# A transformer trunk's convolution inputs moved into Strassen quads, with weight sums made by adding loads

## The chip, the cores and the metric

The kernel runs on one core of one Trainium2 chip. The metric is the time of one execution on the device in microseconds. Its engines work side by side, each through a queue of its own in the order in which instructions were placed there: TensorE (PE; PEld is its weight load), VectorE (DVE), ScalarE (ACT), GpSimd (POOL), and SyncE (SP), which here only issues loads and stores.

## The reference

Two layers over 512 tokens of width 1024. Each has two half-step feed-forward blocks, a mixer between them, and a gated input embedding. The mixer's core:

```python
u = rmsnorm(h, mix_norm[i])
b_g, c_g, v_c, q_c, kv_c, k_r, g_conv, g_mla = jnp.split(u @ w_in[i], split_pts, axis=-1)
y_conv = short_conv_branch(b_g, c_g, v_c, conv_w[i], w_conv_out[i])
y_mla = mla_branch(q_c, kv_c, k_r, q_norm[i], kv_norm[i], w_uq[i], w_ukv[i], w_mla_out[i], cos, sin)
merged = jax.nn.sigmoid(g_conv) * y_conv + jax.nn.sigmoid(g_mla) * y_mla
h = h + merged @ w_o[i]
...
z = c_gate * v                       # short_conv_branch; zp is z with two zero rows ahead
y = conv_w[0] * zp[:, 0:seq]         # plus taps 1 and 2
return (b_gate * y) @ w_conv_out
```

The convolution's inputs B, C and V are 512 columns of `w_in` each; the two gates are 1024 each.

## The kernel before

Activations lie as columns by tokens: `h` is eight tiles of 128 x 512. Everything is computed in float32 through a split: a value is cast to a high part (`wh` for weights, on ScalarE) and the rest is taken on VectorE (`wl`), and a product is made of three matmuls (high times high, high times low, low times high). A block of eight 128 x 128 weight tiles is 128 x 1024, 512 KB. `Stream.raw` loads such a block into a buffer `st` (ten of them) on SP's queue; `Stream.split` makes `wh`, `wl` from it (four of each). A plain projection (`proj`) of 128 output columns uses eight tiles and 24 matmuls of 512 columns.

Some weights are multiplied by Strassen's method in Winograd's form. A quad covers four blocks of 128 output columns; it takes four blocks of weights (`a11`, `a21`, `a22`, `a12`) and makes seven products, numbered 1 to 7, instead of eight. A product is 24 matmuls of 256 columns (half of the tokens). `Quad.part(j)` gives the weights of product j: four of the seven are sums of blocks, made on VectorE (1024 columns each). Products 1, 6, 7 and 4 gather in one PSUM bank `b`, 5 and 3 in `c`, 2 in `a`; after products 1, 5 and 6 ScalarE copies the bank away (`c1`, `c5`, `c6`), after the others VectorE adds bank and copies, and `done` finishes a quarter. Products 5, 7, 6 and 4 need differences of the activations: `Halved.row(j, xs)` makes, for each of four rows, x and y on ScalarE, and t and u (two halves of 256 columns each) and their splits on both engines. Product 5 needs the t of all four rows.

A mixer `m0` or `m1` runs in this order: two projections `kvp`, the rotary key `krp` (its weights need a memset on GpSimd), the sum for its norm (`m0ps`) and from it r (`rms`), three q projections, then four times C, V and B projections with the convolution of that block and one row of `Halved`, then four quads `g0` to `g3` for the gates, with the convolution's output (`conv_out`) between products from the second on, then attention. The Tile framework's scheduler places instructions on each queue from the order of the program and its own estimates; `issue_after(ins)` puts what a block traces on the engine of `ins` behind it. Names such as `wl100` number the splits over the whole program.

## Time and profile before

| | |
|---|---|
| Median of 3 runs | 2277.63 us (2277.48 to 2277.65) |
| The profiled execution | 2277.8 us, span 2275.7 us |
| TensorE's granted clock in it | 0.999 |
| Busy: PE, PEld, DVE, ACT, POOL | 2266.7, 2058.0, 1816.1, 1163.2, 38.1 us |
| DMA | 223.28 MB, mean 98 GB/s |

A row of a timeline gives the start in microseconds, the busy time, engine, line, operation, the tiles written and read, and how often it follows itself; in brackets the idle time ahead of it and who ended it. Engines overlap the end of one instruction with the start of the next, so the distance of two starts is the pace, and the busy time is a little longer.

### The profile page before, as it was taken

How to read it: one execution, taken by the hardware profiler on the slowest of the kernel's cores; microseconds unless marked ns; L12 is line 12 of the kernel's file. 1: busy time of each engine (PE TensorE's matmuls, PEld its weight loads, DVE VectorE, ACT ScalarE, POOL GpSimd, SP SyncE). 2: the span in 40 equal slices, each digit the busy share in tenths (PEclk: the TensorE clock that was granted, in tenths of full speed). 3: DMA queues.
4: the chain of work that ended last, by engine and by line, in shares of the span. 5: the costliest groups of instructions: out<-in, count | busy, mean ns of one | idle time of the engine just before them, and what ended most of it. 6: DMA issues, size and time to landing. Idle time of an engine off the chain costs nothing.

```text
span 2275.7 us, 34817 instructions
## 1 busy us (share of the span) xinstructions
PE 2266.7 (100%) x14206; PEld 2058.0 (90%) x14206; DVE 1816.1 (80%) x2544; ACT 1163.2 (51%) x1751; POOL 38.1 (2%) x42
## 2 busy tenths in 40 slices
PE   9999999999999999999999999999999999999998
PEld 8999988899888999998899999888998889999987
DVE  8877778877877988877798887767878689878766
ACT  7444445456745644444664444454567465444444
POOL 0000000000200000000000000000001000000000
PEclk9999999999999999999999999999999999999999
DMA  5333343134121333333223333422331214333321
GB/s 195 112 112 95 105 130 102 55 113 130 47 66 56 103 112 111 94 120 122 91 80 97 112 93 118 119 87 74 103 121 47 75 38 138 103 103 93 121 93 38
DMA packets 63375, 223.28 MB, mean 98 GB/s; under 512 B 7280, under 2 KB 7280, under 8 KB 63216
## 3 DMA queue, kind: packets, MB, share of 16 engines
q1 hardware_dynamic: 62640, 220.28, 30.7%
q8 instruction: 111, 1.82, 0.3%
q10 hardware_dynamic: 576, 0.79, 0.1%
q14 instruction: 48, 0.39, 0.1%
HBM read 218.94 MB, written 2.10 MB: 97 GB/s over the span
## 4 chain that ended last, share of the span: by engine, by line
PE 98%; DVE 1%; ACT 0%; issue 0%; DVEq 0%; ACTq 0%
PE a0pd L217 2%; PE a1pd L217 2%; PE b0pd L217 2%; PE b1pd L217 2%; PE b1pd L218 2%; PE b0pd L218 2%; PE a1pd L218 2%; PE a0pd L218 2%; PE b0pd L219 2%; PE a1pd L219 2%; PE a0pd L219 2%; PE b1pd L219 2%; PE m0mop L217 1%; PE m1mop L218 1%; PE m0mop L218 1%; PE e0gp L219 1%
## 5 line engine op out<-in xcount | busy, mean ns | idle before, releaser
L70 ACT CAST wh<-st 128x1024 fp32r<-128x1024 f32 (+1 forms) x458 | 476.8, 1044 | 567.2 <-issue 62.7
L71 DVE TENSOR_TENSOR wl<-st,wh 128x1024 fp32r<-128x1024 f32 (+1 forms) x459 | 555.1, 1211 | 155.0 <-ACT wh L70 154.2
L70 ACT CAST wh<-s 128x1024 fp32r<-128x1024 f32 x98 | 103.0, 1051 | 132.6 <-DVE s L151 8.9
L71 DVE TENSOR_TENSOR wl<-s,wh 128x1024 fp32r<-128x1024 f32 x98 | 119.3, 1218 | 13.5 <-ACT wh L70 13.5
L154 DVE TENSOR_TENSOR st<-st,s 128x1024 f32<-128x1024 f32 x49 | 59.9, 1222 | 1.2
L151 DVE TENSOR_TENSOR s<-s,st 128x1024 f32<-128x1024 f32 x49 | 59.7, 1218 | 0.2
L157 DVE TENSOR_TENSOR st<-st,st 128x1024 f32<-128x1024 f32 x49 | 59.6, 1217 | 0.1
L146 DVE TENSOR_TENSOR s<-st,st 128x1024 f32<-128x1024 f32 x49 | 59.6, 1216 | 0.1
L563 DVE SCALAR_TENSOR_TENSOR h<-b1pd,h 128x512 f32<-128x512 f32 x40 | 27.5, 688 | 10.4 <-PE b1pd L219 10.4
L563 DVE SCALAR_TENSOR_TENSOR h<-b0pd,h 128x512 f32<-128x512 f32 x40 | 27.5, 687 | 9.1 <-PE b0pd L219 9.1
L563 DVE SCALAR_TENSOR_TENSOR h<-a1pd,h 128x512 f32<-128x512 f32 x40 | 27.5, 687 | 7.6 <-PE a1pd L219 7.5
L563 DVE SCALAR_TENSOR_TENSOR h<-a0pd,h 128x512 f32<-128x512 f32 x40 | 27.4, 685 | 6.4 <-PE a0pd L219 6.4
L107 POOL MEMSET wh<- 128x256 f32 x4 | 1.1, 312 | 1189.7 <-DVE wl L71 1189.7
L988 ACT ACTIVATE e1g<-e1pg,e1r 128x512 f32<-128x512 f32 (+1 forms) x9 | 5.4, 641 | 11.9 <-PE e1pg L950 11.9
L992 DVE TENSOR_TENSOR e1g<-e1g,e1in 128x512 f32<-128x512 f32 (+1 forms) x9 | 5.7, 628 | 7.3 <-ACT e1g L988 7.3
L117 DVE TENSOR_TENSOR kl<-st,kh 128x512 fp32r<-128x512 f32 x8 | 5.3, 688 | 7.4 <-ACT kh L116 7.4
L882 DVE TENSOR_TENSOR m1g<-m1mop,m1g 128x512 f32<-128x512 f32 x8 | 5.5, 689 | 5.9 <-PE m1mop L219 5.9
L882 DVE TENSOR_TENSOR m0g<-m0mop,m0g 128x512 f32<-128x512 f32 x8 | 5.5, 689 | 5.5 <-PE m0mop L219 5.5
L300 ACT ACT_TABLE_LOAD x7 | 9.0, 1283 | 0.1
L287 DVE TENSOR_TENSOR e1acc<-e1acc,e1sq 128x512 f32<-128x512 f32 x7 | 4.8, 691 | 4.8 <-ACT e1sq L286 4.3
L709 DVE TENSOR_TENSOR m1g<-m1cop,m1g 128x512 f32<-128x512 f32 x8 | 5.5, 687 | 2.0 <-PE m1cop L219 2.0
L709 DVE TENSOR_TENSOR m0g<-m0cop,m0g 128x512 f32<-128x512 f32 x8 | 5.5, 687 | 2.0 <-PE m0cop L219 2.0
(11249 smaller groups left out, 8792.5 us busy)
## 6 DMA issues: line engine op xcount, KB each, us to landing
st<-in_weights SPq DMA_DIRECT2D x406, 512.0 KB, 3.5
h<-in_x SPq DMA_DIRECT2D x8, 256.0 KB, 5.3
st<-in_weights SPq DMA_DIRECT2D x7, 256.0 KB, 5.3
out<-e1d SPq DMA_DIRECT2D x4, 256.0 KB, 2.1
out<-fh SPq DMA_DIRECT2D x3, 256.0 KB, 2.2
e0pi<-in_p SPq DMA_DIRECT2D x2, 256.0 KB, 3.7
e1pi<-in_p SPq DMA_DIRECT2D x2, 256.0 KB, 3.7
fg<-in_final_row SPq DMA_DIRECT2D x2, 256.0 KB, 4.4
```

The lines of the kernel that those rows point to most:

```text
L70: self.nc.scalar.copy(hi[:, w], src[:, w])
L71: last = self.nc.vector.tensor_tensor(lo[:, w], src[:, w], hi[:, w].bitcast(F32), ALU.subtract)
L146: tt(self.s, self.a21, self.a22, ALU.add)
L151: tt(self.s, self.s, self.a11, ALU.subtract)
L154: tt(self.a12, self.a12, self.s, ALU.subtract)
L157: tt(self.a11, self.a11, self.a21, ALU.subtract)
L217: nc.tensor.matmul(ps, wh, vh, start=first, stop=False)
L218: nc.tensor.matmul(ps, wh, vl, start=False, stop=False)
L219: nc.tensor.matmul(ps, wl, vh, start=False, stop=last)
L563: nc.vector.scalar_tensor_tensor(h[m], ps, 0.5, h[m], ALU.mult, ALU.add)
L709: nc.vector.tensor_tensor(gates[m], ps, gates[m], ALU.mult)
L882: nc.vector.tensor_tensor(t, mla_ps[m], t, ALU.mult)
```

## The change

The convolution's C, V and B columns become quads 0, 1 and 2 of the mixer, ahead of the gates (quads 3 to 6), so 12 projections become 21 products. All four rows of `Halved` are made before that, and the q projections stand between the first products. The mixer's quads use a new class: three of their four weight sums are made by loading a block a second time with addition into the buffer that holds another one, on GpSimd's queue. [...] In each later quad product 5 comes ahead of product 1.

```diff
+class Added(Quad):
+    def __init__(self, W, quarters):
...
+        for q in ("a11", "a21", "a22", "a12"):
+            self.at[q] = len(W.halves)
+            setattr(self, q, W.raw(quarters[q]))
+        self.s = self.a21
+        self.add(self.s, "a22")
+
+    def add(self, t, q):
+        self.W.nc.gpsimd.dma_start(out=t, in_=self.W.src[self.at[q]], accum_op=ALU.add)
+
+    def part(self, j):
+        W = self.W
+        if j == 1:
+            res = W.split(self.a11)
+            self.add(self.a11, "a21")
+            return res
+        if j == 5:
+            res = W.split(self.s)
+            self.add(self.s, "a11")
+            return res
+        if j == 3:
+            W.nc.vector.tensor_tensor(self.a12, self.a12, self.s, ALU.add)
+        return W.split({2: self.a12, 3: self.a12, 6: self.s, 7: self.a11, 4: self.a22}[j])
...
-        qt = lat_scale(lat_in(o_q, QL, "q"), "q")
-        kvt = lat_norm(*kvt, "kv")
         krt = rope(krn, cosT, sinT, name + "kr")
-        ys = Halved("mix", l, name)
...
+        ys = Halved("mix", l, name, True)
+        rows = []
+        for k in range(KD // 2):
+            _, last = ys.row(k, xs)
+            rows.append((last, split_to.cast))
         r2 = G(name + "r2")
         nc.vector.tensor_tensor(r2, r, r, ALU.mult)
-        for k in range(CONV // P):
-            ps = proj(W.col("w_in", l, o_c + k * P, D), xs, f"{name}Cp{k}")
...
-            yc.append(split(y, f"{name}yc{k}"))
-            ys.row(k, xs)
-            if k == 1:
-                qt = lat_norm(*qt, "q", SCALE)
...
+        def columns(n):
+            c0 = (o_c, o_v, o_b)[n] if n < N_CONV else o_gc + 4 * (n - N_CONV) * P
+            return [[c0 + (2 * a_ + w) * P for w in range(2)] for a_ in range(2)]
+
+        def conv(n, f, c, src, t):
...
+            if n == 0:
+                nc.vector.tensor_tensor(t, src, r2[:, at].unsqueeze(1).to_broadcast([P, 2, H]), ALU.mult)
+                cs[f, c] = t
+            elif n == 1:
+                for w, k in blocks:
+                    nc.vector.tensor_tensor(zs[k][:, at], src[:, w, :], cs[f, c][:, w, :], ALU.mult)
...
+            else:
+                nc.vector.tensor_tensor(t, src, r[:, at].unsqueeze(1).to_broadcast([P, 2, H]), ALU.mult)
...
-        step = Sevens("w_in", l, name + "g", ys.ys,
-                      lambda n: [[o_gc + (4 * n + 2 * a_ + w) * P for w in range(2)] for a_ in range(2)], gate).step
-        for j in (1, 2, 5, 6, 3):
-            step(0, j)
-        n_last = KD // 2 - 1
+        step = Sevens("w_in", l, name + "g", ys.ys, columns, gate, Added).step
+        step(0, 1)
+        q_block(0)
+        step(0, 2)
+        q_block(1)
+
+        with tc.issue_after(rows[0][0]), tc.issue_after(rows[0][1]):
+            q_block(2)
+        kvt = lat_norm(*kvt, "kv")
+        qt = q_ts, q_sq.parts()
+        with tc.issue_after(rows[1][0]), tc.issue_after(rows[1][1]):
+            step(0, 5)
+        with tc.issue_after(rows[3][0]), tc.issue_after(rows[3][1]):
+            for n, j in ((1, 1), (1, 2), (0, 6), (0, 3)):
+                step(n, j)
+        n_last = N_CONV + KD // 2 - 1
         for n in range(n_last):
...
-            order = [(n + 1, 1), (n, 7), (n + 1, 5), (n, 4)]
-            order += [(n + 1, j) for j in ((6, 2, 7, 3, 4) if n + 1 == n_last else (2, 6, 3))]
+            order = [(n + 1, 5), (n, 7)] + ([(n + 1, 1)] if n else []) + [(n, 4)]
+            order += [(n + 1, j) for j in ((6, 2, 7, 3, 4) if n + 1 == n_last else (2, 6, 3) if n else (6, 3))]
```

How this moves instructions, in layer 0. First VectorE's queue after r. `kvt`, `kvacc` and `kval` are the kv scaling and its sum, `krs` and `krn` the rotary key, `qt` and `qacc` the q scaling and its sum. Before:

```order
L662 TENSOR_TENSOR m0krs_3707<-m0krp_3655,m0krs_3707 64x512
L664 TENSOR_TENSOR m0krn_3706<-m0krs_3707,m0r_3685 64x512 x2
L637 TENSOR_TENSOR m0qt0_3805<-m0qp0_3712,m0r_3685 128x512
L71 TENSOR_TENSOR wl101_3921<-st74_3918,wh101_3920 128x1024
L637 TENSOR_TENSOR m0qt1_3809<-m0qp1_3743,m0r_3685 128x512
L287 TENSOR_TENSOR m0qacc_3807<-m0qacc_3807,m0qsq_3811 128x512
```

Now, from the same rotary key on (`krt` its rotation, t0 and u0 the first row):

```order
L695 TENSOR_TENSOR m0krs_3707<-m0krp_3655,m0krs_3707 64x512
L697 TENSOR_TENSOR m0krn_3706<-m0krs_3707,m0r_3685 64x512 x2
L650 TENSOR_TENSOR m0krt1_3712<-m0krn_3706,cosT_132 128x512
L651 TENSOR_TENSOR m0krt2_3713<-m0krt2_3713,sinT_133 128x512
L429 TENSOR_TENSOR m0t0_3722<-m0x0_3721 128x256
L652 TENSOR_TENSOR m0krt1_3712<-m0krt1_3712,m0krt2_3713 128x512
L445 TENSOR_TENSOR m0t0_3722<-m0y0_3727,m0x0_3721 128x256
L447 SCALAR_TENSOR_TENSOR m0u0_3728<-m0t0_3722,m0x0_3721 128x256
L448 SCALAR_TENSOR_TENSOR m0u0_3728<-m0u0_3728,m0y0_3727 128x256
L241 TENSOR_TENSOR m0t0l_3726<-m0t0_3722,m0t0h_3725 128x512
L241 TENSOR_TENSOR m0u0l_3736<-m0u0_3728,m0u0h_3735 128x512
L71 TENSOR_TENSOR wl100_3950<-st75_3947,wh100_3949 128x1024
```

The split of q block 2's weights (`wl100`) now stands behind the rotation and row 0; rows 1 and 2, the kv norm (`m0kvr`, `m0kvt`) and the split `wl101` of product 5 follow, and then the end of row 3 and what stands ahead of the split `wl102` (quad 1's product 1):

```order
L241 TENSOR_TENSOR m0t3l_3780<-m0t3_3776,m0t3h_3779 128x512
L241 TENSOR_TENSOR m0u3l_3790<-m0u3_3782,m0u3h_3789 128x512
L705 TENSOR_TENSOR m0r2_3793<-m0r_3685 128x512
L711 TENSOR_TENSOR m0qt0_3875<-m0qp0_3844,m0r_3685 128x512
L515 TENSOR_TENSOR m0g0c1_3842<-m0g0a_3879,m0g0c1_3842 128x512
L711 TENSOR_TENSOR m0qt1_3941<-m0qp1_3910,m0r_3685 128x512
L735 TENSOR_TENSOR m0g0c1_3842<-m0g0c1_3842,m0r2_3793 128x512
L711 TENSOR_TENSOR m0qt2_3977<-m0qp2_3946,m0r_3685 128x512
L318 TENSOR_TENSOR m0qacc_3877<-m0qacc_3877,m0qsq_3943 128x512
L71 TENSOR_TENSOR wl102_4042<-st76_4031,wh102_4041 128x1024
```

The q scalings, which stood right behind the rotary key, now stand behind all four rows, and `wl102` behind them. On TensorE's queue, after q block 2, the convolution's first projection followed before:

```order
L219 MATMUL m0qp2_3774<-m0x7h_3582,wl98_3778 128x512
L296 MATMUL m0kvps_3823<-m0kvah_3702,ones_76 128x512
L297 MATMUL m0kvps_3823<-m0kval_3703,ones_76 128x512
L217 MATMUL m0Cp0_3847<-m0x0h_3534,wh99_3850 128x512
L218 MATMUL m0Cp0_3847<-m0x0l_3535,wh99_3850 128x512
```

Now product 5 of quad 0 (bank `m0g0c`) follows, which reads the rows; this is its end and what comes after it:

```order
L491 MATMUL m0g0c_3999<-m0t3l_3780,wh101_4000 128x256
L491 MATMUL m0g0c_3999<-m0t3h_3779,wl101_4001 128x256
L491 MATMUL m0g1b_4040<-m0x0h_3534,wh102_4041 128x256
L491 MATMUL m0g1b_4040<-m0x0l_3535,wh102_4041 128x256
L491 MATMUL m0g1a_4072<-m0x4h_3561,wh103_4073 128x256
L491 MATMUL m0g1a_4072<-m0x4l_3562,wh103_4073 128x256
L491 MATMUL m0g0b_3812<-m0u0h_3735,wh104_4104 128x256
L491 MATMUL m0g0b_3812<-m0u0l_3736,wh104_4104 128x256
L491 MATMUL m0g1b_4040<-m0x0h_3534,wl102_4042 128x256
```

Two matmuls each of three products (quad 1's 1 and 2, quad 0's 6), then the rest of the first, which reads `wl102`. GpSimd's queue held only the memset for the rotary key's weights at this place before:

```order
masks.py:199 ISA
masks.py:199 AFFINE_SELECT ident_80<-ident_80 128x128
L107 MEMSET wh95_3658 128x4x64 x2
L814 TENSOR_SCALAR m0s00e0_5613<-m0s00e0_5613,m0s00sm_5616 128x128
L814 TENSOR_SCALAR m0s00e0_5613<-m0s00e0_5613,m0s00sm_5616 128x384
```

Now adding loads stand around it (`st70` is s of quad 0, `st77` that of quad 1, `st81` that of quad 2; `st69` and `st76` are a11 of quads 0 and 1):

```order
L176 DMA st70_3805<-in_weights 128x1024
L107 MEMSET wh95_3658 128x4x64 x2
L176 DMA st77_4033<-in_weights 128x1024
L176 DMA st69_3803<-in_weights 128x1024
L176 DMA st81_4341<-in_weights 128x1024
L176 DMA st70_3805<-in_weights 128x1024
```

The fifth of them adds a11 to s of quad 0 for its product 6, and waits until the split of product 5 has read s.

## The prediction

> **What bounds the kernel now.** I read the page's busy line first, then the shares of the chain that ended last, TensorE's clock by slice, and the waits of TensorE alone.

> ```profile
> PE 2266.7 (100%) x14206; PEld 2058.0 (90%) x14206; DVE 1816.1 (80%) x2544; ACT 1163.2 (51%) x1751; POOL 38.1 (2%) x42
> PE 98%; DVE 1%; ACT 0%; issue 0%; DVEq 0%; ACTq 0%
> PEclk9999999999999999999999999999999999999999
> PE idle L325 <- DVE hpi L255: 1.0, 1, 1.0
> ```

> TensorE is the bound from end to end: its only wait is 1.0 us at the start. So a microsecond of matmuls removed is a microsecond won, and a microsecond in which TensorE waits is lost for good, since no later stage has slack on it. VectorE, at 80%, is the engine to watch.

> **The matmuls removed.** Two stretches give their pace (columns: stretch, length, then busy time and count of PE, PEld, DVE, ACT, POOL, the granted clock, DMA share, GB/s). The first holds the twelve convolution projections and two matmuls of a norm, the second six Strassen products of gates.

> ```profile
> 384.37:450.15 65.78, 65.78 (x291) 54.43 (x290) 52.90 (x75) 30.48 (x43) 0.00 (x0) 1.00 0.18 56
> 470.60:487.90 17.30, 17.30 (x147) 17.30 (x146) 15.29 (x18) 10.12 (x17) 0.00 (x0) 1.00 0.45 149
> ```

> Without the norm's 0.46 us, twelve projections take 65.3 us, 5.44 each; a product takes 17.3 / 6 = 2.88 us. Three quads of seven products replace the twelve: 21 x 2.88 = 60.5 us. The gain is 4.8 us in a layer, 9.6 in two. (24 matmuls of half the width cost more than half a projection, 2.88 against 2.72: in the second stretch weight loads are busy all the time.)

> **The rows, moved ahead of the convolution.** Before, a row of differences (x, t, u, y) was made after each third projection, four times in 65 us in which TensorE needed none of them. Now all four stand on VectorE and ScalarE between the mixer's norm r and the split `wl102`, and product 5 of the first quad reads them. On TensorE, after the matmuls of r's sum, stand product 1, q block 0, product 2, q block 1, q block 2 with the kv norm's two matmuls, product 5, then two matmuls each of three products, then the rest of the first of these, which reads `wl102`. When would TensorE want that, and when can VectorE give it?

> ```profile
> 367.55 0.40 PE L217 MATMUL m0qp<-m0x0h,wh 128*128 128x512 f32 x1
> ...
> 373.19 1.29 DVE L637 TENSOR_TENSOR m0kvt<-m0kvp,m0r 128x512 f32<-128x512 f32 x2
> 374.39 1.21 DVE L71 TENSOR_TENSOR wl<-st,wh 128x1024 fp32r<-128x1024 f32 x1
> 375.52 0.68 DVE L287 TENSOR_TENSOR m0kvacc<-m0kvacc,m0kvsq 128x512 f32<-128x512 f32 x1
> 376.89 0.69 DVE L210 TENSOR_TENSOR m0kval<-m0kvacc,m0kvah 128x512 fp32r<-128x512 f32 x1 [0.69 <-ACT m0kvah L209]
> 377.50 0.68 DVE L662 TENSOR_TENSOR m0krs<-m0krp,m0krs 64x512 f32<-64x512 f32 x1
> 378.22 1.38 DVE L664 TENSOR_TENSOR m0krn<-m0krs,m0r 64x512 f32<-64x512 f32 x2
> 379.61 0.69 DVE L637 TENSOR_TENSOR m0qt<-m0qp,m0r 128x512 f32<-128x512 f32 x1
> ```

> Up to r (first used at 373.19) both orders are the same. TensorE's next work would start at 367.55, as there, and want `wl102` after 2.88 + 5.44 + 2.88 + 5.44 + 0.46 + 5.44 + 2.88 and six matmuls of 0.12: 26.1 us, at 393.7. VectorE's paces, from one start to the next:

> ```profile
> 405.11 0.42 DVE L397 TENSOR_TENSOR m0t<-m0x 128x256 f32<-128x256 f32 x1
> 405.44 0.42 DVE L413 TENSOR_TENSOR m0t<-m0y,m0x 128x256 f32<-128x256 f32 x1
> 405.89 0.42 DVE L414 TENSOR_TENSOR m0u<-m0t,m0x 128x256 f32<-128x256 f32 x1
> 406.35 0.42 DVE L415 TENSOR_TENSOR m0u<-m0y,m0u 128x256 f32<-128x256 f32 x1
> ...
> 408.34 0.68 DVE L210 TENSOR_TENSOR m0t0l<-m0t,m0t0h 128x512 fp32r<-128x512 f32 x1
> 408.94 0.68 DVE L210 TENSOR_TENSOR m0u0l<-m0u,m0u0h 128x512 fp32r<-128x512 f32 x1
> 409.55 0.68 DVE L677 TENSOR_TENSOR m0c<-m0Cp,m0r 128x512 f32<-128x512 f32 x1
> ...
> 447.63 1.22 DVE L151 TENSOR_TENSOR s<-s,st 128x1024 f32<-128x1024 f32 x1
> 448.77 0.74 DVE L685 SCALAR_TENSOR_TENSOR m0y<-m0z,cols,m0y 128x510 f32<-128x510 f32 x1
> 449.43 1.22 DVE L154 TENSOR_TENSOR st<-st,s 128x1024 f32<-128x1024 f32 x1
> ```

> So 0.60 for 512 columns, 0.66 with a gain column, 1.14 for 1024, and 0.33 + 0.45 + 0.46 + 0.43 + 2 x 0.60 = 2.87 for a row. From 373.19 to the end of `wl102` VectorE now has: sixteen 512-wide operations (the kv scaling and its sum, rotary, kv norm, r2, the q and first-product evictions), 9.6; the rotary key, 2.1 (377.50 to 379.61); four rows, 11.5; `wl100` and `wl101`, 2.3; the two kv scalings with a gain, 1.3; `wl102` itself, 1.2. That is 28.0 us, so `wl102` is there at 401.2 at the earliest, 7.5 us late even if VectorE never waits.

> It will wait, since it hands work to ScalarE and back, as the 0.69 in its kval row shows. ScalarE's paces:

> ```profile
> 384.94 0.69 ACT L300 ACTIVATE m0kvr<-m0kvps,eps_t 128x512 f32<-128x512 f32 x1
> 385.52 0.62 ACT L286 ACTIVATE m0qsq<-m0qt 128x512 f32<-128x512 f32 x1
> 386.04 0.62 ACT L301 ACTIVATE m0kvt<-m0kvr 128x512 f32<-128x512 f32 x1
> 386.56 0.68 ACT L302 ACTIVATE m0kvms<-m0kvps,eps_t 128x512 f32<-128x512 f32 x1
> 387.13 0.62 ACT L209 CAST m0qah<-m0qacc 128x512 fp32r<-128x512 f32 x1
> 387.78 2.51 ACT L613 COPY m0krt<-m0krn 32x512 f32<-32x512 f32 x4
> 390.31 1.05 ACT L70 CAST wh<-st 128x1024 fp32r<-128x1024 f32 x1
> ```

> Going down both queues with these (0.6 for 512 columns, 1.0 for a cast of weights, 2.5 for the four rotary copies), VectorE waits 1.6 us for the squares and cast of the kv sum (no split lies between them any more), 1.3 for the rotary copies, 0.7 for `wh100`, 0.9 for y1 of row 1, and about 0.8 for a square of q, which on ScalarE stands behind the cast `wh104`: 5.3 in all, `wl102` at 406.5. TensorE stands in pieces: about 2 us for `wl100` at q block 2, 3 for `wl101` and 2.5 for `m0t3l` in product 5, 5.4 for `wl102`. Of this term I take 406.5 - 393.7 = 12.8 us a layer; its lower end is 7.5. Layer 1 has the same distance from r's sum to r's use (6.1 us, as 367.55 less two matmuls to 373.19):

> ```profile
> 1494.55 0.39 PE L296 MATMUL m1ps<-m1ah,ones 128*128 128x512 f32 x1
> 1500.65 1.29 DVE L637 TENSOR_TENSOR m1kvt<-m1kvp,m1r 128x512 f32<-128x512 f32 x2
> ```

> **Adding loads for sums.** Per layer 21 adding loads go out on GpSimd's queue; of the 16 sums that VectorE made for four quads of gates, 7 are left for seven quads, 9 x 1.14 = 10 us less of VectorE. That gain lies beside a TensorE that never waits there: worth nothing by itself. Against it come nine more weight splits (9 x 1.14) and more evictions: in quads 1 and 2 of the convolution VectorE has 18.9 and 18.4 us of work and 3.2 for the q norm, beside 40.3 us of matmuls. It runs full and TensorE will touch it; I take 1.0 us (`wl117`). Twenty-two MB more of loads, over a DMA share of 0.18 to 0.45, cost nothing; SP issues as many loads as before. The memset for the rotary key's weights now stands behind one adding load on GpSimd's queue (two in layer 1); their plain loads were issued several splits earlier, which hides this; uncovered, it would cost one landing. Quad 2's first adding load stands there ahead of quad 0's second; its tile's plain load goes out when `wl100` frees a buffer, near 387, and lands 3.5 us later, before quad 0's can start at 395: no cost.

> An adding load itself is in no row. The nearest are plain loads of the same 512 KB:

> ```profile
> st<-in_weights SPq DMA_DIRECT2D x406, 512.0 KB, 3.5
> DMA to landing us min/median/max: 3.1/3.5/11.4
> ```

> It also reads the tile it adds to, so between 3.5 and 11.4 us; I take 5, nearer the median. Product 6 needs the sum that is issued when product 5's split is done. In quad 0 about 7 us lie between (396 to 403), so nothing is lost at 5. In quad 1 only two splits lie between; there the sum for product 3 and two more splits queue on VectorE behind the load, then the eviction of product 7, for which product 4 of quad 0 waits in the same PSUM bank: 1.4 us at 5, nothing at 3.5, and 3.6 more at the first place and 5.7 at the second if it is 11.4. In the gates' quads four splits lie between and nothing is lost.

> [...]

> **The sum.** Per layer -4.8 + 12.8 + 1.0 + 1.4 = +10.4; two layers +20.8. The profiled execution took 2277.8 us (span 2275.7), 0.2 above the median of the runs, 2277.63. So 2277.8 + 20.8 = 2298.6, and I say 2298.

> **Rivals.**
> - It is faster. One mechanism decides it: VectorE's queue after r keeps ahead of TensorE, so nothing is lost and 2277.8 - 9.6 = 2268 remains. For it: TensorE never waits now. Against it: 28.0 us of VectorE work at measured paces have 20.5 us (373.19 to 393.7). It turns faster only where `wl102` comes less than 4.8 us late, by 398.5. Chance 0.05, and 0.05 for something close to no change.
> - VectorE runs without the waits on ScalarE: 7.5 us a layer lost, 2 x 2.7 more, 2283. For it: some waits may overlap; against: the 0.69 row. Chance 0.12.
> - Adding loads take twice what I took or more. At 11.4 us another 9.3 a layer, less the 1.0 at `wl117` that this covers: 2315. Only the longest plain load speaks for it. Chance 0.13.
> - TensorE's clock falls while it waits. It is full in every slice of a trace in which TensorE never waits, so no row excludes it. If one product's worth of work after the waits runs at half pace, 2.88 us a layer: 2304. Chance 0.15. [...]
> - As summed, 2298: chance 0.50.

> The range 2283 to 2314 takes in the second and fourth rivals and most of the third. A measurement of this kernel can tell about 0.2% (4.6 us) from no change: faster 0.05, same 0.05, slower 0.90.

> **What would show it.** In the trace after: products at 2.88 us; TensorE's waits, now 1.0 us, near 30 us, on `wh`/`wl` splits and on `m0t2l`, `m0t3l` between q block 2 and the second quad's first product; the stretch from the mixer's first product to the end of product 6 some 13 us longer than its matmuls; almost none in the gates. Adding loads should land in about 5 us with no wait named on them over 2 us. I am wrong if product 5 follows q block 2 with no wait, or if the waits lie on adding loads instead.

## The result and the profile after

The changed kernel takes 2307.99 us, median of four runs (2306.05 to 2310.39), against 2277.56 for the kernel before on the same chip: ratio 1.0134, interval 1.0117 to 1.0152. The profiled execution is one of 2306.2 us (span 2304.3), 28.6 us of span more than before. From the page, busy times and TensorE's clock in 40 slices:

```profile
PE 2272.5 (99%) x14638; PEld 2079.8 (90%) x14638; DVE 1829.7 (79%) x2578; ACT 1190.6 (52%) x1787; POOL 74.9 (3%) x84
...
PEclk9999999999999999999999999989999999999999
```

TensorE has fewer columns to multiply and is busy 5.8 us longer: some of its matmuls ran slower, and one slice shows a clock below full. Where it stood in layer 0 (engine, tile and line that waited, who ended the wait: us in total, times, longest):

```profile
PE m0g0c L491 <- DVE wl L71: 2.7, 1, 2.7
PE m0g1b L491 <- DVE wl L71: 2.4, 2, 1.6
PE m0qp L248 <- ACT wh L70: 1.4, 1, 1.4
PE m0g1b L491 <- ACT wh L70: 1.1, 1, 1.1
PE m0g0b L491 <- DVE m0g0c L515: 1.1, 1, 1.1
PE m0g1a L491 <- ACT wh L70: 0.9, 1, 0.9
PE m0g0b L491 <- ACT wh L70: 0.9, 1, 0.9
PE m0g0c L491 <- DVE m0t3l L241: 0.4, 1, 0.4
PE m0g0c L491 <- ACT m0t3h L240: 0.4, 1, 0.4
```

These are the tiles that were named: splits of weights, `m0t3l`, and with 1.1 us the eviction `m0g0c`, on which the forecast's term for the first quad's last product rests. A ledger of what was lost where comes from five starts of TensorE's timeline: the mixer's first product, the first matmul behind `wl102`, products 5 and 3 of quad 1, and the first matmul of attention:

```profile
367.58 0.28 PE L491 MATMUL m0g0b<-m0x0h,wh 128*128 128x256 f32 x1
...
406.32 0.58 PE L491 MATMUL m0g1b<-m0x0h,wl 128*128 128x256 f32 x1 [1.60 <-DVE wl L71]
...
418.62 0.28 PE L491 MATMUL m0g1c<-m0t0h,wh 128*128 128x256 f32 x1
...
434.30 0.28 PE L491 MATMUL m0g1c<-m0x4h,wh 128*128 128x256 f32 x1
...
560.68 0.50 PE L248 MATMUL m0h0qr<-m0qn0h,wh 128*128 128x512 f32 x1
```

The last of these in the kernel before:

```profile
547.45 0.50 PE L217 MATMUL m0h0qr<-m0qn0h,wh 128*128 128x512 f32 x1
```

From 367.58 the work ahead of `wl102` is 26.1 us, so 393.7; it went on at 406.32: 12.6 lost. From there to 418.62 stand 66 matmuls of 0.12 and one product, 10.8 us, and it took 12.3: 1.5 lost. From 418.62 to 434.30 stand four products and a norm's matmuls, 12.0 us, and it took 15.7: 3.7 lost. Near 455 another 0.3. That is 18.1, less 4.84 of matmuls saved: 13.2, as 560.68 - 547.45 says. The same sums in layer 1: 12.6, 2.7, 4.6 and 0.3, 20.2, less 4.84, 15.3. From attention on, the two kernels run in step to 0.1 us up to the next layer's mixer, and from its attention to the end.

The 1.5 is a slower clock: no wait stands between the 66 matmuls. Four stretches of layer 0 (columns as in the prediction; the clock stands before the DMA share):

```profile
395.89:399.31 3.42, 3.01 (x15) 2.71 (x14) 3.08 (x8) 2.48 (x4) 0.87 (x1) 0.50 0.58 78
399.31:402.72 3.41, 1.93 (x10) 1.31 (x10) 3.33 (x7) 3.31 (x5) 0.00 (x0) 1.00 0.39 76
402.72:409.55 6.83, 4.36 (x19) 3.77 (x19) 6.75 (x9) 3.40 (x6) 0.86 (x1) 0.50 0.15 20
409.55:416.37 6.82, 6.82 (x59) 6.82 (x59) 4.32 (x7) 4.04 (x5) 0.00 (x0) 1.00 0.69 145
```

At a granted 0.50 the matmuls of 256 columns start every 0.21 us instead of 0.12. The 3.7 is an adding load. VectorE's and GpSimd's rows there:

```profile
417.35 0.86 POOL L176 DMA_DIRECT2D st<-in_weights  x1 [9.64 <-DVE wl L71]
...
419.91 0.69 DVE L735 TENSOR_TENSOR m0g0c<-m0g0c,m0r 128x512 f32<-128x512 f32 x1
424.48 1.23 DVE L189 TENSOR_TENSOR st<-st,st 128x1024 f32<-128x1024 f32 x1 [3.88 <-DMA st<-in_weights]
...
428.20 0.69 DVE L515 TENSOR_TENSOR m0g0c<-m0g0b,m0g0c 128x512 f32<-128x512 f32 x1
```

Sent at 417.35, it landed at 424.45, 7.1 us later. VectorE stood 3.9 us for it with the sum for product 3, and behind that sum waited two splits and the eviction of product 7, which frees the bank for the first quad's last product (TensorE at 428.94).

### The profile page after: what moved, and what is told of

It is laid out like the page before. It is cut to its first block, busy times and chain, and to the rows that moved or that the text cites. A ratio compares the mean times of both kernels' runs of the same rounds, so it can differ in the third digit from the quotient of the medians.

```text
span 2304.3 us, 35901 instructions
## 1 busy us (share of the span) xinstructions
PE 2272.5 (99%) x14638; PEld 2079.8 (90%) x14638; DVE 1829.7 (79%) x2578; ACT 1190.6 (52%) x1787; POOL 74.9 (3%) x84
## 3 DMA queue, kind: packets, MB, share of 16 engines
q8 instruction: 114, 1.87, 0.3%
## 5 line engine op out<-in xcount | busy, mean ns | idle before, releaser
L70 ACT CAST wh<-st 128x1024 fp32r<-128x1024 f32 (+1 forms) x492 | 511.7, 1044 | 571.3 <-issue 59.4
L71 DVE TENSOR_TENSOR wl<-st,wh 128x1024 fp32r<-128x1024 f32 (+1 forms) x493 | 596.8, 1213 | 170.9 <-ACT wh L70 170.1
L70 ACT CAST wh<-s 128x1024 fp32r<-128x1024 f32 x82 | 86.2, 1051 | 105.6 <-DVE s L151 8.9
L71 DVE TENSOR_TENSOR wl<-s,wh 128x1024 fp32r<-128x1024 f32 x82 | 99.9, 1218 | 0.8 <-ACT wh L70 0.8
L176 POOL DMA_DIRECT2D st<-in_weights x42 | 36.8, 878 | 1469.3 <-DVE a1an L538 799.2
L154 DVE TENSOR_TENSOR st<-st,s 128x1024 f32<-128x1024 f32 x41 | 50.2, 1223 | 1.1
L146 DVE TENSOR_TENSOR s<-st,st 128x1024 f32<-128x1024 f32 x41 | 50.1, 1222 | 0.1
L157 DVE TENSOR_TENSOR st<-st,st 128x1024 f32<-128x1024 f32 x41 | 50.0, 1220 | 0.1
L151 DVE TENSOR_TENSOR s<-s,st 128x1024 f32<-128x1024 f32 x41 | 50.0, 1220 | 0.0
L189 DVE TENSOR_TENSOR st<-st,st 128x1024 f32<-128x1024 f32 x14 | 17.1, 1223 | 7.5 <-DMA st<-in_weights 7.3
## 6 DMA issues: line engine op xcount, KB each, us to landing
st<-in_weights SPq DMA_DIRECT2D x406, 512.0 KB, 3.6
st<-in_weights POOLq DMA_DIRECT2D x42, 512.0 KB, 6.0
```

What stands on the lines that cost most here:

```text
L70: self.nc.scalar.copy(hi[:, w], src[:, w])
L71: last = self.nc.vector.tensor_tensor(lo[:, w], src[:, w], hi[:, w].bitcast(F32), ALU.subtract)
L146: tt(self.s, self.a21, self.a22, ALU.add)
L151: tt(self.s, self.s, self.a11, ALU.subtract)
L154: tt(self.a12, self.a12, self.s, ALU.subtract)
L157: tt(self.a11, self.a11, self.a21, ALU.subtract)
```

## The experiments

Theory A joins two terms of the prediction and one of its rivals: the rows in VectorE's queue, adding loads with too few splits between, and a clock that halves behind such waits. B puts the loss on the adding loads, C on too many splits for VectorE and ScalarE.

**Rows ahead of r.** The rows need only h, so they can be written where VectorE idles.

```diff
+        ys = Halved("mix", l, name, True)
+        rows = []
+        for k in range(KD // 2):
+            ...
         r = rms(acc, D, name)
         kvt = lat_scale(pkv, "kv")
...
         krt = rope(krn, cosT, sinT, name + "kr")
-        ys = Halved("mix", l, name, True)
-        ...
```

> The changed kernel, with the four rows of differences written ahead of the mixer's norm r instead of behind the rotary key; they need only h and the gains. Same work, same instructions. VectorE stands idle ahead of r for 10.6 us in layer 1 (1498 to 1512.5) and for 4.7 us in layer 0, against 11.5 us of rows. Theory A (the rows in VectorE's queue between r and wl102 cost 12.6 us a layer at the first quad, and the half clock behind it 1.5 and 2.7): layer 1 loses at most 2 us there and its clock stays full, layer 0 keeps about 7.5 us of it; the 3.7 us a layer at the first quad's last product stay. Layer 1 then stands at -4.8 + 1.5 + 3.7 + 0.3 = +0.7 against before, layer 0 at -4.8 + 8.5 + 3.7 + 0.3 = +7.7: 2286, between 2280 and 2293. Theory B (the adding loads and GpSimd's queue hold the splits up, the rows do not matter): 2306, no change. Theory C (three quads have too many splits for VectorE and ScalarE, wherever the rows stand): the same work has only moved, 2300 to 2306.

Measured: 2279.67 (2276.62 to 2281.39), ratio 1.0009 (1.0000 to 1.0019). So 28 of 30 us lay in the place of the rows; B and C are out as the main cause. In the profiled execution (2276.6) layer 1 stands 1.2 us ahead of before, layer 0 0.6 behind. The time is just under A's range of 2280 to 2293: A let r and all behind it wait for the rows, while r came only some 2 us later in both layers and what followed it was not needed at once; and of the adding load's 3.7 us a layer, which A kept, TensorE's waits there are 0.3 in layer 0 and 2.7 in layer 1. What TensorE still waits for, over 1 us:

```profile
PE m0qps L327 <- ACT m0qah L240: 1.7, 1, 1.7
PE m1g0b L491 <- DVE m1g0c L515: 1.4, 1, 1.4
PE m1g1b L491 <- DVE wl L71: 1.3, 1, 1.3
```

The last two are the adding load's place again.

**Adding loads alone.** The kernel before, with this edit and the signs that go with it (t, u and half of the results are turned):

```diff
-        ys = Halved("mix", l, name)
+        ys = Halved("mix", l, name, True)
...
-                      lambda n: ..., gate).step
+                      lambda n: ..., gate, Added).step
```

> The kernel before, with its convolution left as projections and the old order of products, but with the turned rows and three of four weight sums of the gates' quads made by adding loads. Theory A (adding loads cost only where few splits lie between the load and its use): 2278, up to 2284 if product 6 of the first quad, which here follows product 5 at once, waits up to 3 us a layer. The 10 us of VectorE work that go win nothing. Theory B (the adding loads are what costs): of the 28 us lost at least half, 2290 or more.

Measured: 2281.42 (2280.28 to 2283.12), ratio 1.0017 (1.0007 to 1.0026): A's range, 3.8 us lost. Not by product 6 but by the sum for product 3, which stands in VectorE's queue ahead of row 3 (its row of the timeline); row 3 and a split then come late for TensorE (the waits behind it):

```profile
452.23 1.23 DVE L189 TENSOR_TENSOR st<-st,st 128x1024 f32<-128x1024 f32 x1 [1.79 <-DMA st<-in_weights]
```

```profile
PE m0g0c L491 <- ACT m0t3h L240: 0.8, 1, 0.8
PE m0g1b L491 <- DVE wl L71: 0.7, 1, 0.7
```

The VectorE work that went won nothing, as forecast; it is more than the 10 us of the expectation, twelve sums a layer of 1.14 us, 13.7.

**All sums on VectorE.**

```diff
     def add(self, t, q):
-        self.W.nc.gpsimd.dma_start(out=t, in_=self.W.src[self.at[q]], accum_op=ALU.add)
+        self.W.nc.vector.tensor_tensor(t, t, getattr(self, q), ALU.add)
...
```

Each sum is made right ahead of the split that reads it, that of product 5 into a buffer of its own.

> The changed kernel with the same sums of weights, all made on VectorE, and no adding load. Theory A: the first quad waits longer by the one or two sums that now stand ahead of wl102 and of the split of product 6 (1.14 us each), so 14 to 15 us a layer and 2 at half clock; the wait of 3.7 us at the first quad's last product goes; VectorE, already full in quads 1 and 2 (18.9 and 18.4 us of work and 3.2 of the q norm beside 40.3), gets 6.8 more and TensorE waits some 5 there. Per layer -4.8 + 14.5 + 2 + 5 = +17, 2311, between 2300 and 2320. Theory B (the adding loads are what costs): 2285 or less, since what is left is 10 us fewer matmuls against some VectorE work.

Measured: 2312.06 (2311.41 to 2313.57), ratio 1.0152 (1.0137 to 1.0167), against 2311 by A and 2285 by B. In the trace layer 0 loses 17.2 and layer 1 16.6. The two longest waits of layer 0's first products are longer now, and none names an eviction of the first quad any more:

```profile
PE m0g1b L492 <- DVE wl L71: 4.6, 1, 4.6
PE m0g0c L492 <- ACT wh L70: 4.0, 1, 4.0
```

**Plain loads for adding ones.** One run of the changed kernel.

```diff
-        self.W.nc.gpsimd.dma_start(out=t, in_=self.W.src[self.at[q]], accum_op=ALU.add)
+        self.W.nc.gpsimd.dma_start(out=t, in_=self.W.src[self.at[q]])
```

> The changed kernel with the 42 adding loads turned into plain loads of the same bytes into the same tiles from the same queue at the same places, so the three sums are left out of the weights. It tells whether the 6.0 us to landing (plain loads of SP's queue: 3.6) belong to the addition or to GpSimd's queue. If to the addition: 3.6 to 4 us, the wait at the first quad's last product falls from 3.7 and 4.6 us to 1 or less, and the time by 5 to 8 us, to 2299 to 2304. If to the queue: still 6, and 2306 to 2310.

Measured: 2298.89 in the one run, 0.1 under the range for the addition. The landings of the 42 loads from GpSimd's queue (the answer for the line that issues them), of the changed kernel:

```profile
DMA to landing us min/median/max: 5.1/6.0/9.4
```

and of this one:

```profile
DMA to landing us min/median/max: 3.6/4.0/7.4
```

In the medians the addition costs 2.0 us (6.0 against 4.0), GpSimd's queue 0.4 (SP's plain loads in the changed kernel: 3.6). The stretch from product 5 to product 3 of quad 1, which lost 3.7 and 4.6 us, loses 0.8 and 0.6 here.

**Matmuls that fill the waits.**

```diff
+            for _ in range(fill):
+                nc.tensor.matmul(ps.rearrange("p w t -> p (w t)"), ones, self.whole, start=True, stop=True)
             self.product(ps, d, j)
...
-            step(0, 5)
+            step(0, 5, 12)
...
-                step(n, j)
+                step(n, j, 20 if (n, j) == (1, 1) else 0)
```

> The changed kernel with 32 matmuls of 512 columns per layer that nobody reads (products' own PSUM banks, ahead of their first matmul): 12 ahead of product 5 and 20 ahead of the first product of quad 1, 7.3 us of work where TensorE stood waiting for 10 us. They change no wait's end, so if only the waits count the time stays at 2306 to 2310. If the half clock (matmuls of 256 columns at 0.21 us instead of 0.12 behind the waits, 1.5 us in layer 0, 2.7 in layer 1, 1.4 more at layer 1's next wait) comes from TensorE having stood, it goes, the granted clock returns from 0.993 to 0.998 or more, and the time falls by 3 to 6 us, to 2301 to 2304.

Measured: 2303.11 (2300.67 to 2308.4). The four runs follow the clock: 2300.7 and 2301.3 at a granted 0.998, 2304.9 at 0.996, 2308.4 at 0.994. The changed kernel has 2306.1 and 2306.2 at 0.993, 2309.8 and 2310.4 at 0.990. So the same instructions take up to 8 us more or less, and the clock leaves room for it: 0.004 of 2300 us is 9 us. But the forecast clock came in two runs of four only, and the profiled run is the 2308.4, in which waits of up to 1.9 us were left and the clock fell at other places (0.50 from 428 to 432, where the changed kernel has it full): that filling is the cure is not shown by a trace.

**Waits put into the kernel before**, to see what the clock needs.

```diff
                 nc.scalar.copy(d[j], ps)
+                w = getattr(self, "gaps", {}).get(n) if j == 1 else None
+                if w:
+                    g = G(nn + "gap", F32R)
+                    nc.gpsimd.tensor_copy(g[:, :w], d[j].rearrange("p w t -> p (w t)")[:, :w])
+                    self.behind = nc.tensor.matmul(PS(nn + "gap")[:, :w], ones, g[:, :w], start=True, stop=True).ins
...
```

> The kernel before with 32 waits of TensorE put in, eight in each of the four feed-forward blocks, one every 31 us: behind a product a matmul that nobody reads waits for ScalarE's copy of that product and for a GpSimd copy of 64 to 512 columns of it; an estimated 1 to 2.5 us each, so 2277.8 + 30 to 80. Theory H (the clock halves only behind a window of 3.41 us in which no matmul ran): no wait is that long, the clock stays at 0.999. Theory I (it halves behind a window of 3.41 us in which TensorE stood for more than 1.3 to 1.9 us, as in the traces so far, and comes back behind a busy one): the longer waits are followed by 3.4 or 6.8 us at half clock, those below 1.3 us by none, and waits that a window's edge cuts in two by fewer.

Measured: 2391.34 in the one run, with 32 waits of 2.5 to 5.3 us, 92.9 in all: longer than estimated. The clock is at 0.994: five of the waits are followed by half clock, 27 are not. Three of the five are the longest, of 4.5 to 5.3 us; the other two last 2.6 and 2.7 us and the 27 from 2.5 to 2.9, so among these length does not tell them apart. What does is the grid: the stretches at half clock begin at 72.27, 826.62, 1359.10, 1393.23 and 2011.05 us, whole multiples of 3.413 us from one another, and all the waits but one lie across an edge of that grid (the one, of 2.63 us, lies whole in a window and is followed by half clock). Two neighbours, of 2.53 us (0.79 and 1.74 on the two sides of an edge) and of 2.74 us (0.90 and 1.84), each with the window in which the longer part lies and the next one, cut 0.03 us ahead of the grid:

```profile
1321.57:1324.98 3.41, 1.64 (x13) 1.64 (x14) 3.39 (x4) 1.27 (x3) 0.39 (x1) 1.00 0.23 19
1324.98:1328.39 3.41, 3.41 (x23) 3.08 (x22) 1.72 (x3) 1.35 (x2) 0.00 (x0) 1.00 0.90 287
1355.70:1359.10 3.40, 1.53 (x12) 1.53 (x13) 3.40 (x4) 1.16 (x3) 0.60 (x1) 1.00 0.26 42
1359.10:1362.50 3.40, 3.40 (x17) 3.30 (x17) 0.43 (x2) 0.50 (x1) 0.00 (x0) 0.51 0.83 270
```

TensorE stood 0.1 us longer in the third row's window than in the first's (1.87 against 1.77); the first was followed by a full clock, the third by 0.51. So it is over all 32: ahead of the five TensorE stood 1.88 us or more of a whole window on the grid, and in no window of the 27 more than 1.79. No window in front of the five was free of matmuls (the emptiest had TensorE stand 3.1 us of it), and waits of 2.63 and 2.74 us can empty none, so H falls; I is right in kind, with the figures of the last section.

**Rows ahead, and products in an order with more room.**

```diff
-        step(0, 1)
-        q_block(0)
-        ...
+        q_block(0)
+        step(0, 1)
+        q_block(1)
+        step(0, 2)
+        step(0, 5)
+        q_block(2)
+        with tc.issue_after(last):
+            step(0, 6)
+        ...
-            order = [(n + 1, 5), (n, 7)] + ([(n + 1, 1)] if n else []) + [(n, 4)]
+            order = [(n + 1, 5), (n, 7)] + [(n + 1, 1)] + [(n, 4)]
```

> The changed kernel with the rows ahead of the norm r, and three orders more: the q projections alternate with products 1, 2 and 5 of the first quad; the products of quads 1 and 2 go in the order of the gates' quads (four products between product 5 and product 6, instead of two); the q norm is asked for in quad 2. Same instructions. Theory A (the change loses only by the rows in VectorE's queue, by adding loads with too few splits between, and by the half clock behind such waits): all three go, and what is left is the 9.6 us of matmuls: 2277.6 - 9.6 + about 2 of small waits = 2270, between 2268 and 2274, granted clock 0.999. Theory C (seven quads keep VectorE too full wherever the rows stand): 2277 or more.

Measured: 2279.81 (2279.03 to 2280.78), ratio 1.0010 (1.0001 to 1.0019): outside A's range. In the trace layer 1 gains 3.4 us as forecast, layer 0 loses 5.2. There VectorE is through its rows 12.6 us after r, in layer 1 4.2 us after it: it idles less ahead of r, and one wait, for y of row 3, takes 3.65 us (its row of the timeline). Two of TensorE's waits are over 1 us. The one of 1.3 us, at 396.2, is ended by VectorE's work on the rotary key (`m0krs`), as it would be if the key's projection still held the bank of PSUM (argued, not shown). The other, of 2.1 us, is for a cast of weights; the granted clock of this run is 0.997, against 0.999 before:

```profile
385.14 0.43 DVE L445 TENSOR_TENSOR m0t<-m0y,m0x 128x256 f32<-128x256 f32 x1 [3.65 <-ACT m0y L444]
```

```profile
PE m0g1b L491 <- ACT wh L70: 2.1, 1, 2.1
PE m0g1c L491 <- DVE m0krs L698: 1.3, 1, 1.3
```

**The same with all sums on VectorE** (the edit of the third experiment).

> The kernel rows_even with all weight sums made on VectorE, no adding load. If adding loads are a gain once they are given time: VectorE has 37.3 us of work in quads 1 and 2 beside 40.3 of matmuls, and six more sums of 1.14 us make it 44, so TensorE waits some 4 us a layer there, 1 or 2 more in the first quad and as much at half clock: 2278, between 2273 and 2285. If they are worth nothing: 2270 like rows_even.

Measured: 2292.56 (2292.19 to 2293.14), ratio 1.0066 (1.0052 to 1.0079), 12.8 us above rows_even and 7.6 above the range. Beside waits of 3.7 and 4.2 us in quad 2 there is one of 4.3 at the first kv projection, for a split, which neither rows_even nor the expectation has. In the trace VectorE is busy without a break there from 331.6 to 356 and makes that split at 356.1, behind work for the rotary tables that in rows_even stands behind a split at 348.4; why the scheduler placed it so is open. With it and the lower clock (0.994 in this run, 0.997 in rows_even) 6.8 of the 12.8 us are lost ahead of layer 0's mixer. Of the rest layer 1 loses 6.9 and layer 0 gains 1.2. So adding loads are worth some 7 us in a layer that nothing else disturbs; the 12.8 as a whole are not shown to be theirs.

**Norms put off.**

```diff
+                if (n_, j_) == (2, 6):
+                    with tc.issue_after(W.last_split):
+                        kvt = lat_norm(*kvt, "kv")
+                if (n_, j_) == (3, 6):
+                    with tc.issue_after(W.last_split):
+                        qt = lat_norm(*qt, "q", SCALE)
+                if (n_, j_) == (4, 6):
+                    ...
+                        krt = rope(krn, cosT, sinT, name + "kr")
```

> The kernel rows_even with three things put off that nothing needs before attention: the kv norm to quad 2, the q norm to quad 3, the rotary key to quad 4, each behind a weight split on VectorE. Same instructions. In rows_even layer 1 had gained 3.4 us and layer 0 lost 5.2: its VectorE, 5 us behind r by then, was busy without a break from 385 to 405, with some 9 us of these three. Theory A (only VectorE's backlog ahead of quad 1 was left in layer 0, and the half clock behind it): TensorE's want of wl104 at 394 is met (8.8 us of VectorE work from 384.3), layer 0 gains 3 to 4 us as layer 1 does, clock 0.999: 2277.6 - 7 = 2270.5, between 2268.5 and 2274. If it is something else in layer 0 (the loads, ScalarE), it stays near 2279.

Measured: 2274.06 (2272.76 to 2275.24), ratio 0.9986 (0.9977 to 0.9995). Layer 1 gains 5.1, layer 0 loses 0.4. What held layer 0, in the timeline of ScalarE and VectorE, and then the wait of TensorE that came of it:

```profile
384.08 1.05 ACT L70 CAST wh<-st 128x1024 fp32r<-128x1024 f32 x1 [2.42 <-DMA st<-in_weights]
385.03 0.72 ACT L444 ACTIVATE m0y<-h,cols 128x512 f32<-128x512 f32 x1
...
385.78 0.43 DVE L445 TENSOR_TENSOR m0t<-m0y,m0x 128x256 f32<-128x256 f32 x1 [3.67 <-ACT m0y L444]
```

```profile
PE m0g0b L491 <- ACT m0g0c L510: 2.9, 1, 2.9
```

A cast that waited 2.42 us for an adding load stood ahead of y of row 3, VectorE stood 3.67 us for that y, and what is behind it came later. It is the wait of 3.65 us that rows_even had already.

**That cast behind the rows.**

```diff
-        with tc.issue_after(last):
+        with tc.issue_after(last), tc.issue_after(cast):
             step(0, 6)
...
-        with tc.issue_after(last):
+        with tc.issue_after(last), tc.issue_after(cast):
             step(0, 3)
```

> The kernel settled, with product 6 and product 3 of the first quad held behind the last cast of the rows on ScalarE's queue too (before, on VectorE's only). One pair changes places there in layer 0: y of row 3 now comes ahead of the cast wh102, which waits for an adding load. In settled VectorE stood 3.67 us for that y, and TensorE 2.9 us for the first quad's copy and 1.5 in three pieces behind it; layer 1 had its whole gain (5.1 us), layer 0 none (+0.4). If a queue held up by an adding load is what was left: layer 0 gains 3.5 to 4.5 us, 2270.0, between 2269 and 2272. If layer 0 has another bound (its VectorE backlog): 2273 to 2274.

Measured: 2269.04 (2268.55 to 2269.86), ratio 0.9963 (0.9949 to 0.9976), 8.6 us faster than before and 39 faster than the changed kernel. VectorE's row 3 in the timeline, and then all that TensorE waits for in the whole execution:

```profile
382.24 0.42 DVE L445 TENSOR_TENSOR m0t<-m0y,m0x 128x256 f32<-128x256 f32 x1 [0.19 <-ACT m0y L444]
```

```profile
PE m0g1c L491 <- DVE wl L71: 1.4, 1, 1.4
PE idle L356 <- DVE hpi L286: 1.0, 1, 1.0
```

What the program asks for is the work of the changed kernel; only places in the queues differ. Layer 0 gains 3.4 us, layer 1 5.1.

## Why the prediction was right, and where its sizes were off

Direction and range held: slower, 2308 in 2283 to 2314. The point, 2298, was 10 us low against the median and 8 against the profiled execution, from which the parts are read. By its own steps:

- *The matmuls removed, 4.8 a layer.* Right: with the waits gone layer 1 gains 5.1 (the 0.3 more were not followed up).
- *The rows, 12.8 a layer.* Right: 12.6 in both layers. `wl102`, forecast to end at 406.5, began at 405.04 and ended at 406.3; waits at `wl100` 1.4 (forecast 2), at `wl101` 2.7 (3), then `m0t3l` and `wl102` in smaller pieces. The sum came out closer than its two parts, and that is luck: from 373.22 to 406.26 VectorE waited 4.0 us (forecast 5.3) and the rest took 29.0 (forecast 28.0). Rows ahead of r took the loss away.
- *`wl117`, 1.0.* 0.3: VectorE kept up better in quads 1 and 2.
- *The first quad's last product, 1.4.* 3.7 and 4.6. The mechanism was right, the landing was not: I took 5 us, and it was 6.0 in the median and 7.1 at this place. The prediction's own arithmetic gives 1.4 + 2.1 = 3.5 at 7.1. The plain loads, at 4.0, show that the 2 us are the addition's.
- *The clock, a rival at 0.15.* It came true beside the sum and not in place of it: 27 us of the span at half clock in two layers. It cost 1.5 and 2.7 us behind `wl102`, and a part of layer 1's 4.6. I had priced it at 2.9 a layer, with a half pace that no trace of before shows; the trace after shows a granted 0.50, and 0.21 us a matmul instead of 0.12. That several rivals can hold at once was the mistake in how the chances were laid out: here a late landing made a wait (3.9 us of VectorE), waits were followed by half clock, and all pushed one way.
- *What would show it.* I said waits near 30 us and no adding load named over 2 us. The waits are 22 beside the 1.0 at the start, since a part of the loss is slow matmuls, and VectorE's wait for an adding load is 3.9.

Two terms that were too small (by 2.3 and 3.2 us at the last product, by 1.5 and 2.7 of clock, which the sum had at nothing) less 1.4 of `wl117` and 0.4 of the rows make the 8 us between 20.8 forecast and 28.6 measured.

## What to carry to other kernels

When work is moved ahead of a bound engine's stage, sum the feeder's queue from the moment its inputs exist to the moment of the first use, and compare with the bound engine's own work in between: that gave 12.8 for a measured 12.6. Then look for idle time of the feeder ahead of that moment, and for what in its queue nothing needs yet; moving rows, products and norms turned the same work from 30 us lost to 8.6 won. An instruction that waits for a slow load should stand in no queue ahead of work that others need, on ScalarE (2.42 us in settled) as little as on VectorE (3.88 in the changed kernel).

## What was not expected of the hardware

Standing in pieces was enough: in the window from 399.31 on, with ten matmuls, no wait is longer than 0.92 us, and half clock follows. No half clock followed 27 of the 32 waits of 2.5 us and more in gaps, all of them cut by a window's edge, where TensorE stood 1.79 us or less of each window, while 1.88 was followed by half clock. Runs of one kernel differ by 4 us (changed kernel, granted clock 0.990 to 0.993) to 8 us (filled, 0.994 to 0.998); what makes their clocks differ is not shown.

An adding load of 512 KB from GpSimd's queue landed 2.0 us later than a plain one from it (medians of 6.0 in the changed kernel and 4.0 in plain_loads; 5.5 to 6.5 in the other traces with adding loads), and that one 0.4 later than SP's 3.6.
